# Halves of whole weight tiles made two products ahead in a hybrid decoder layer

## Chip, cores and metric

One core of a Trainium2 chip. The metric is the device time of one execution, in microseconds. A line of code is named L153 and so on, as the profile counts them in the kernel before; TensorE is PE, VectorE is DVE, ScalarE is ACT, GpSimd is POOL and SyncE is SP in the rows.

## What is computed

One decoder layer over 1024 tokens with 1024 channels in float32, with d = 512 for the two branches and 2816 for the up projection:

```python
h = rmsnorm(x, g_mix); z = h @ w_in
a = a_val * sigmoid(a_gt)
a = causal_dwconv(a, conv_a_w) + conv_a_b                 # 31 taps
y_a = silu(layernorm(a, ln_a_g, ln_a_b)) @ w_a_out
y_b = (sc_b * causal_dwconv(sc_c * sc_v, conv_b_w)) @ w_b_out   # 3 taps
x = x + (g_a * y_a + g_b * y_b) @ w_o                     # g_a, g_b: sigmoids from z
u = rmsnorm(x, g_ffn) @ w_up
f = gelu(causal_dwconv(u[:, :2816], conv_f_w) + conv_f_b) * u[:, 2816:]
x = x + f @ w_down
x = x + sigmoid(rmsnorm(x, g_ple) @ w_ple_gate) * (p @ w_ple)
return rmsnorm(x, g_final)
```

## The kernel before

Activations lie channels by tokens, in tiles of 128 channels by 1024 tokens. Every float32 operand of a product is written as a high half `hi` (a cast on ACT, L130) and a low half `lo = x - hi` (a subtraction on VectorE, L131), both by `halve`; a product is then three matmuls (hi·hi, hi·lo, lo·hi; `mm`, L143 to L153). SBUF is one pool of 54 tiles of 4 KB per partition (`NBIG`), from which activations, raw weights and their halves are taken.

The stages follow each other on TensorE: the start with the p @ w_ple products; the input projection as pairs of weight tiles (`Pair`, matmuls L601, copies L610, L617 and L623), each made with sums of halves of the weights; the w_b products of the second branch, one whole weight tile of 8 blocks (128x128) for two output tiles (`half_products`), evicted by a multiplication with a gate (L870); between the first and the third of them the LayerNorm of the first branch, with column sums by matmuls with a matrix of ones (`cs_mm`, L380 and L381), subtraction of the mean (L878), squares (L391) and their sum (L399), square root (L360), reciprocal (L363), scaling (L888), SiLU (L889); the four w_a products with evictions L902 and L903 and halves `m` of the result; the eight o products (`o_mm`, L928 to L930), evicted by an addition to x (`o_add`, L938), scaled (L939), squared (L945, L948) and summed by columns (`o_rstd`, L968); the up projection in pairs again; the down projection in three chunks of 8, 8 and 6 blocks (additions L1086); and the gate stage, w_pg products in three segments of 448, 320 and 256 columns (`Item`, gate L1125 and L1128). A whole product of 8 blocks and 1024 columns is 48 matmuls of 512 columns.

Weights go through the `Loader` (L155 to L276). `use` lists every use of a weight in the order of the program and adds up its cost in passes: 48 for a whole tile of 8 blocks, 12 for a use of a pair. At each use `get` first requests loads on SP's queue, in the order of cost less AHEAD, as long as they lie at most AHEAD passes ahead (`whole` tiles L207; of pairs L213, L217, and L222 to L224 with accumulating loads by POOL, L226). Then it writes the halves (`split`) of those weights that lie at most SPLIT passes ahead. Loads named in `held` wait: "up" is held from the o stage's start, and let go (`ld.held.clear()`, L1005) behind the product and evictions of o's last pair for the first 512 tokens.

An engine runs its instructions in order. The orders of TensorE and SP are written out in the program; on ACT, VectorE and POOL a scheduler orders them at build time, except in the start and the gate stage, where ACT and VectorE are written out too. So where a weight's halves stand on ACT and VectorE follows from where `get` writes them and from what the scheduler makes of it.

Of the kernel before, what the change touches and what calls it, by code (L numbers as in the profile page):

```python
# [13 lines left out]
PE = mybir.EngineType.PE  # L14
ACT = mybir.EngineType.Activation
DVE = mybir.EngineType.DVE
SP = mybir.EngineType.SP
# [5 lines left out]
DC = 512  # L23
# [41 lines left out]
NBIG = 54  # L65


AHEAD = {"whole": 120, "r": 110, "q": 100, "s": 150, "late": 200}
SPLIT = 40


@with_exitstack
def trunk_kernel(ctx, tc, xT, pT, par, w_in, w_a, w_b, w_o, w_up, w_dn, w_ple, w_pg, outT):
# [48 lines left out]
    def slot(name, dt=F32):  # L122
        return big.tile([P, T], dt, tag="u", name=name)
# [31 lines left out]
    class Loader:  # L155
# [39 lines left out]
        def sort(self):  # L195
            self.loads.sort(key=lambda x: self.cost[x[0]] - AHEAD[x[1]])
            self.pending = list(self.splits)
# [32 lines left out]
        def split(self, key, arg):  # L230
# [13 lines left out]
                hi, lo = split(t, "w_" + key[-1])  # L244
            self.done[key] = (hi, lo)

        def fetch(self, n):

            while self.loaded < n:
                self.load(*self.loads[self.loaded][1:])  # L250
                self.loaded += 1
# [6 lines left out]
        def get(self, load=True):  # L258
            i = self.at
            self.at += 1  # L260
            now = self.cost[i]
            while load and self.loaded < len(self.loads):
                n, kind, key, _ = self.loads[self.loaded]
                if n > i and (key[0] in self.held or self.cost[n] - now > AHEAD[kind]):
                    break
                self.fetch(self.loaded + 1)
            while self.pending and (
                self.pending[0][0] <= i or load and self.cost[self.pending[0][0]] - now <= SPLIT
            ):
                self.split(*self.pending.pop(0)[1:])  # L270
            key, side = self.uses[i]
            w = self.done[key]
            if side is not None and key[-1] != "q":
                c = slice(side * DC, (side + 1) * DC)
                w = tuple(x[:, c] for x in w)
            return w  # L276

    def block_order(n, head=1):

# [31 lines left out]
    ld = Loader()  # L311
# [20 lines left out]
        ld.add(w_pg[j], 8, kind="late")  # L332
    ld.sort()

    with tc.manual_schedule(engines={PE, SP}):
        ps_stack = ExitStack()
        psp = ps_stack.enter_context(tc.tile_pool(name="psp", bufs=8, space=PSUM))

# [216 lines left out]
        def right_sums(a0, a1, b0, b1):  # L555

            t13, t24 = slot("t13"), slot("t24")
            nc.vector.tensor_sub(t13[:, H0], a0, a1)
            nc.vector.tensor_sub(t13[:, H1], b1, a1)
            nc.vector.scalar_tensor_tensor(t24[:, H0], t13[:, H0], -1.0, b1, ALU.mult, ALU.subtract)  # L560
            nc.vector.scalar_tensor_tensor(t24[:, H1], t24[:, H0], -1.0, b0, ALU.mult, ALU.subtract)
            return t13, t24

        def sum_halves(t13, t24, name):

            out = {}
            hi, lo = split(t13, name + "s")
            out[5], out[7] = (hi[:, H0], lo[:, H0]), (hi[:, H1], lo[:, H1])
            hi, lo = split(t24, name + "t")
            out[6], out[4] = (hi[:, H0], lo[:, H0]), (hi[:, H1], lo[:, H1])  # L570
            return out
# [241 lines left out]
        for i in range(4):  # L813
            xa, xb = xr[i], xr[4 + i]
            r = sum_halves(*right_sums(xa[:, H0], xa[:, H1], xb[:, H0], xb[:, H1]), "hs")
# [14 lines left out]
        for n, (p, m) in enumerate(in_order):  # L830
            if m == 1:
                kind, i = IN_PAIRS[p]
# [109 lines left out]
        def o_square(i, c):  # L942
            r = xs[i, c.start]
            sq = slot("sq")
            nc.scalar.activation(sq, r, AF.Square)  # L945
            if c.start in osum:
                acc = osum[c.start]
                nc.vector.tensor_add(acc, acc, sq)  # L948
            else:
                osum[c.start] = sq  # L950

        def o_plain(i):

            hi, lo = split(xg[i, 0], "xgp")
            rows[i][1], rows[i][2] = (hi[:, H0], lo[:, H0]), (hi[:, H1], lo[:, H1])
# [8 lines left out]
        def o_rstd(c, cs):  # L964
            ps = bank()
            for i, q in enumerate(HALVES):
                for x, y in ((0, i == 0), (1, False)):
                    nc.tensor.matmul(ps, ones_d, cs[x][:, q], start=y, stop=x == 1 and i == 1)  # L968
            sqrt(rstd[:, c], ps)
            inverse(rstd[:, c])  # L970
# [24 lines left out]
        for i in (2, 3):  # L995
            for c in HALVES:
                for q in range(2):
                    if (i, c, q) == (3, H1, 1):
                        o_rstd(H0, cs_0)
                    o_mm(i + 4 * q, c, range(KD), True, True)  # L1000
                    o_add(i, q, c)
                if c is H0:
                    o_plain(i)
                if i == 3 and c is H0:
                    ld.held.clear()  # L1005
                    o_square(i, c)
                    cs_0 = cs_split(osum[0])
                    o_sums(2)
                elif i == 3:
                    o_sums(i)  # L1010
                    o_square(i, c)
                else:
                    o_square(i, c)
# [147 lines left out]
        with tc.manual_schedule(engines={ACT, DVE}):  # L1161
# [80 lines left out]
            fs, r = stats[-1]  # L1242
# [83 lines left out]
```

## Time and profile before

| | before |
|---|---|
| median of 3 runs | 1506.3 us (1506.01 to 1506.63) |
| profiled execution, its own time | 1504.43 us |
| its span | 1502.7 us |
| mean granted TensorE clock | 0.952 |
| TensorE busy | 1356.9 us, 90% of the span |
| VectorE busy | 913.4 us, 61% |
| ACT busy | 526.3 us, 35% |
| DMA | 216.64 MB, mean 144 GB/s |

The profile is of one execution; its own time is 1.9 us under the median of the runs, and 1.7 us lie around its span. A granted clock of 1.00 is 2.4 GHz, one of 0.50 is 1.2 GHz. "Idle before" is the time in which an engine did nothing ahead of an instruction, with the work whose end let it go. Some matmul records are missing in a trace, so counts of them are a little low.

### The profile page before, as it was taken

What the parts mean: (1) busy time and instruction counts of PE and PEld (TensorE: products, weight loads), DVE (VectorE), ACT (ScalarE), POOL (GpSimd) and SP (SyncE); (2) the same over time, 40 slices, a digit from 0 to 9 for tenths busy, and PEclk for the clock granted to TensorE, in tenths of its full rate; (3) what the DMA queues carried; (4) which work ended last, traced back from release to release, by engine and by line L of the source; (5) the groups of instructions that cost most, each with busy time, mean ns of one, the idle gap of its engine ahead of it and who ended that gap; (6) DMA issues with size and microseconds to landing.
All of it is one profiled execution on the core that took longest, in us unless ns stands there. A gap on an engine that the chain in (4) does not pass through costs nothing.

```text
span 1502.7 us, 15409 instructions
## 1 busy us (share of the span) xinstructions
PE 1356.9 (90%) x5930; PEld 1116.9 (74%) x5930; DVE 913.4 (61%) x1036; ACT 526.3 (35%) x691; POOL 181.7 (12%) x247
## 2 busy tenths in 40 slices
PE   9989999999839787768999999999979999997697
PEld 7778887888737566556888888888858888886586
DVE  7979999994463535355666666666674341254376
ACT  7442432344331124233433333333352120133244
POOL 1111321221000001013222222222000000000011
PEclk9999999999968989888999999999989999999798
DMA  9564876786732204048777777777392230112022
GB/s 340 146 137 123 247 180 147 189 215 185 275 144 79 89 0 140 28 134 188 182 182 182 182 178 180 182 182 182 106 381 81 90 107 11 61 53 84 18 77 78
DMA packets 84905, 216.64 MB, mean 144 GB/s; under 512 B 9696, under 2 KB 14048, under 8 KB 84832
## 3 DMA queue, kind: packets, MB, share of 16 engines
q1 hardware_dynamic: 52992, 140.15, 28.8%
q0 software_dynamic: 31840, 75.51, 21.8%
q8 instruction: 46, 0.75, 0.2%
q14 instruction: 27, 0.22, 0.1%
HBM read 159.00 MB, written 36.70 MB: 130 GB/s over the span
## 4 chain that ended last, share of the span: by engine, by line
PE 80%; DVE 11%; ACT 4%; issue 2%; DMA 2%; SPq 0%; DVEq 0%; ACTq 0%
PE ps L601 43%; PE ps L153 31%; PE ps L930 2%; PE ps L928 2%; DVE acc L676 2%; PE ps L929 2%; DVE wlo L131 1%; ACT whi L130 1%; DVE w_s_lo L131 1%; DVE ssq L399 1%; DMA x<-x_d 1%; DVE sc_cv L676 1%; DVE rstd L363 0%; DVE lrstd L363 0%; DVE w_r_lo L131 0%
## 5 line engine op out<-in xcount | busy, mean ns | idle before, releaser
L676 DVE SCALAR_TENSOR_TENSOR acc<-a,prm,acc 128x1023 f32<-128x1023 f32 (+14 forms) x120 | 151.7, 1264 | 1.7
L153 PE MATMUL ps<-f_hi,whi 128*128 128x512 f32 x352 | 109.2, 392 | 9.4 <-ACT whi L130 9.4
L153 PE MATMUL ps<-f_hi,wlo 128*128 128x512 f32 x352 | 108.9, 391 | 0.1
L153 PE MATMUL ps<-f_lo,whi 128*128 128x512 f32 x352 | 108.9, 390 | 0.0
L131 DVE TENSOR_TENSOR w_s_lo<-s,w_s_hi 128x1024 fp32r<-128x1024 f32 x76 | 92.5, 1219 | 16.1 <-DMA gate_d<-gate 8.4
L1086 DVE TENSOR_TENSOR x<-ps,x 128x512 f32<-128x512 f32 x46 | 29.6, 685 | 104.9 <-PE ps L153 104.9
L226 POOL DMA_DIRECT2D s<-s x76 | 66.6, 876 | 184.5 <-DMA s<-s 66.9
L153 PE MATMUL ps<-xp_hi,whi 128*128 128x448 f32 (+2 forms) x192 | 66.5, 347 | 24.1 <-ACT whi L130 22.9
L623 ACT COPY u<-ps 128x512 f32<-128x512 f32 x38 | 22.4, 589 | 182.5 <-PE ps L601 182.5
L131 DVE TENSOR_TENSOR wlo<-raw,whi 128x1024 fp32r<-128x1024 f32 (+2 forms) x55 | 63.0, 1160 | 34.9 <-ACT whi L130 17.8
L153 PEld LDWEIGHTS ps<-f_hi,whi 128*128 128x128 f32 x352 | 66.5, 189 | 23.6 <-ACT whi L130 9.9
L130 ACT CAST w_s_hi<-s 128x1024 fp32r<-128x1024 f32 x76 | 79.7, 1050 | 2.9 <-DMA s<-s 2.0
L601 PE MATMUL ps<-xgp_hi,w_r_hi 128*128 128x512 f32 x176 | 69.5, 395 | 12.0 <-ACT w_r_hi L130 12.0
L153 PEld LDWEIGHTS ps<-f_hi,wlo 128*128 128x128 f32 x352 | 66.2, 188 | 14.5 <-DVE wlo L131 0.9
L153 PEld LDWEIGHTS ps<-f_lo,whi 128*128 128x128 f32 x352 | 66.4, 189 | 14.0
L928 PE MATMUL ps<-m,whi 128*128 128x512 f32 x128 | 54.6, 426 | 22.8 <-ACT whi L130 22.8
L676 DVE SCALAR_TENSOR_TENSOR fg<-u_t,neg_f,fg 128x1023 f32<-128x1023 f32 (+1 forms) x44 | 56.4, 1283 | 28.3 <-ACT fg L670 27.6
L601 PE MATMUL ps<-xgp_hi,w_r_lo 128*128 128x512 f32 x176 | 69.4, 394 | 0.2 <-DVE w_r_lo L131 0.2
L601 PE MATMUL ps<-xgp_lo,w_r_hi 128*128 128x512 f32 x176 | 69.2, 393 | 0.0
L153 PE MATMUL ps<-xp_hi,wlo 128*128 128x448 f32 (+2 forms) x192 | 66.1, 344 | 3.1 <-DVE wlo L131 2.8
L601 PE MATMUL ps<-xgs_hi,w_s_hi 128*128 128x512 f32 x176 | 68.5, 389 | 0.0
L601 PE MATMUL ps<-xgs_lo,w_s_hi 128*128 128x512 f32 x176 | 68.5, 389 | 0.0
(263 smaller groups left out, 3366.5 us busy)
## 6 DMA issues: line engine op xcount, KB each, us to landing
s<-s POOLq DMA_DIRECT2D x76, 256.0 KB, 4.4
raw_r<-w_up SPq DMA_DIRECT2D x22, 512.0 KB, 5.2
s<-w_up SPq DMA_DIRECT2D x44, 256.0 KB, 3.0
s<-w_up SPq DMA_DIRECT2D x22, 512.0 KB, 6.0
s<-w_up POOLq DMA_DIRECT2D x44, 256.0 KB, 6.5
f_d<-v_t POOLq DMA_DIRECT2D x22, 512.0 KB, 5.9
f<-f_d SPq DMA_DIRECT2D x22, 512.0 KB, 5.2
s<-w_in SPq DMA_DIRECT2D x32, 256.0 KB, 3.0
```

The lines of the kernel that those rows point to most:

```text
L130: nc.scalar.copy(hi, src)
L131: nc.vector.tensor_sub(lo, src, f32(hi))
L153: nc.tensor.matmul(ps[:, :step], wt[:, b], xt[:, t : t + step], start=f, stop=l)
L226: nc.gpsimd.dma_start(dst, src, accum_op=ALU.add)
L399: nc.vector.tensor_add(self.acc[:, c], self.acc[:, c], sq[:, c])
L601: nc.tensor.matmul(ps, wt[:, b], xt, start=f, stop=l, skip_group_check=True)
L623: nc.scalar.copy(self.e[:, H1], self.b)
L676: nc.vector.scalar_tensor_tensor(dst[:, s:], src[:, : T - s], w(k), dst[:, s:], ALU.mult, ALU.add)
L928: nc.tensor.matmul(ps, whi[:, b], hi, start=first and k == ks[0], stop=False)
L929: nc.tensor.matmul(ps, whi[:, b], lo, start=False, stop=False)
L930: nc.tensor.matmul(ps, wlo[:, b], hi, start=False, stop=last and k == ks[-1])
L1086: nc.vector.tensor_add(x1[j][:, c], ps, x1[j][:, c])
```

## The change

Four things. SPLIT is now 100 passes for whole tiles (it was 40) and stays at 40 for pairs, with the condition that the raw tile has already been requested (`ready`). AHEAD for whole tiles goes from 120 to 150. The part of `get` that requests and splits is a method `advance` of its own, and it is called once more where the hold on up's loads ends. SP's order is no longer written out in the program but left to the scheduler.

```diff
--- before.py
+++ after.py
@@ -65,8 +65,8 @@
 NBIG = 54
 
 
-AHEAD = {"whole": 120, "r": 110, "q": 100, "s": 150, "late": 200}
-SPLIT = 40
+AHEAD = {"whole": 150, "r": 110, "q": 100, "s": 150, "late": 200}
+SPLIT = {True: 100, False: 40}
 
 
 @with_exitstack
@@ -244,6 +244,9 @@
                 hi, lo = split(t, "w_" + key[-1])
             self.done[key] = (hi, lo)
 
+        def ready(self, key):
+            return key in self.raw
+
         def fetch(self, n):
 
             while self.loaded < n:
@@ -258,22 +261,26 @@
         def get(self, load=True):
             i = self.at
             self.at += 1
+            self.advance(i, load)
+            key, side = self.uses[i]
+            w = self.done[key]
+            if side is not None and key[-1] != "q":
+                c = slice(side * DC, (side + 1) * DC)
+                w = tuple(x[:, c] for x in w)
+            return w
+
+        def advance(self, i, load=True):
             now = self.cost[i]
             while load and self.loaded < len(self.loads):
                 n, kind, key, _ = self.loads[self.loaded]
                 if n > i and (key[0] in self.held or self.cost[n] - now > AHEAD[kind]):
                     break
                 self.fetch(self.loaded + 1)
-            while self.pending and (
-                self.pending[0][0] <= i or load and self.cost[self.pending[0][0]] - now <= SPLIT
-            ):
+            while self.pending:
+                n, key, arg = self.pending[0]
+                if n > i and not (load and self.cost[n] - now <= SPLIT[key[0] == "whole"] and self.ready(key)):
+                    break
                 self.split(*self.pending.pop(0)[1:])
-            key, side = self.uses[i]
-            w = self.done[key]
-            if side is not None and key[-1] != "q":
-                c = slice(side * DC, (side + 1) * DC)
-                w = tuple(x[:, c] for x in w)
-            return w
 
     def block_order(n, head=1):
 
@@ -332,7 +339,7 @@
         ld.add(w_pg[j], 8, kind="late")
     ld.sort()
 
-    with tc.manual_schedule(engines={PE, SP}):
+    with tc.manual_schedule(engines={PE}):
         ps_stack = ExitStack()
         psp = ps_stack.enter_context(tc.tile_pool(name="psp", bufs=8, space=PSUM))
 
@@ -1003,6 +1010,7 @@
                     o_plain(i)
                 if i == 3 and c is H0:
                     ld.held.clear()
+                    ld.advance(ld.at - 1)
                     o_square(i, c)
                     cs_0 = cs_split(osum[0])
                     o_sums(2)
```

TensorE's order is the same. At three places the others stand as follows; `whi` and `wlo` are the halves of a whole weight tile, `raw` the loaded tile, `cs_hi` and `cs_lo` the halves of what is summed over columns.

First, ACT at the end of the input projection and at the LayerNorm's sums. Before:

```order
L623 COPY u_2858<-ps 128x512
L783 ACTIVATE gate<-gate,prm 128x512
L783 ACTIVATE gate<-ps,prm 128x512
L130 CAST s_hi<-s 128x1024
L783 ACTIVATE gate<-gate,prm 128x512
L130 CAST s_hi<-s 128x1024
L130 CAST cs_hi<-acc 128x1024
L391 ACTIVATE ssq<-acc 128x1024
L391 ACTIVATE sq<-acc 128x1024 x3
L130 CAST cs_hi<-ssq 128x1024
L130 CAST whi<-raw 128x1024
L360 ACT_TABLE_LOAD
```

and now:

```order
L130 CAST whi<-raw 128x1024
L630 COPY u_2860<-ps 128x512
L790 ACTIVATE gate<-gate,prm 128x512
L790 ACTIVATE gate<-ps,prm 128x512
L130 CAST s_hi<-s 128x1024
L790 ACTIVATE gate<-gate,prm 128x512
L130 CAST s_hi<-s 128x1024
L130 CAST cs_hi<-acc 128x1024
L130 CAST whi<-raw 128x1024
L398 ACTIVATE ssq<-acc 128x1024
L398 ACTIVATE sq<-acc 128x1024 x3
L130 CAST cs_hi<-ssq 128x1024
```

The second w_b's cast stood behind the second column sum's (`cs_hi<-ssq`); it is now ahead of the last copy of the pairs, and the third's stands ahead of the squares. In VectorE's order at the same place, before:

```order
L870 TENSOR_TENSOR gate<-ps,gate 128x512 x4
L878 TENSOR_TENSOR acc<-acc,ps 128x512 x8
L399 TENSOR_TENSOR ssq<-ssq,sq 128x1024 x3
L131 TENSOR_TENSOR cs_lo<-ssq,cs_hi 128x1024
L131 TENSOR_TENSOR wlo<-raw,whi 128x1024
L870 TENSOR_TENSOR gate<-ps,gate 128x512 x4
L363 RECIPROCAL lrstd<-lrstd 128x512 x2
L888 TENSOR_TENSOR acc<-acc,lrstd 128x1024 x4
```

and now:

```order
L877 TENSOR_TENSOR gate<-ps,gate 128x512 x4
L885 TENSOR_TENSOR acc<-acc,ps 128x512 x8
L877 TENSOR_TENSOR gate<-ps,gate 128x512 x2
L131 TENSOR_TENSOR wlo<-raw,whi 128x1024
L406 TENSOR_TENSOR ssq<-ssq,sq 128x1024 x2
L877 TENSOR_TENSOR gate<-ps,gate 128x512
L406 TENSOR_TENSOR ssq<-ssq,sq 128x1024
L877 TENSOR_TENSOR gate<-ps,gate 128x512
L131 TENSOR_TENSOR cs_lo<-ssq,cs_hi 128x1024
L131 TENSOR_TENSOR wlo<-raw,whi 128x1024
L370 RECIPROCAL lrstd<-lrstd 128x512 x2
L877 TENSOR_TENSOR gate<-ps,gate 128x512
```

The evictions `gate<-ps` of the second product (two, then one and one) now stand among the additions of squares, ahead of the column sum's low half.

Second, VectorE at the first square sum of o (`x<-ps` is an eviction of a product, `sq<-sq` the addition of squares, `t` the first of the sums for up). Before:

```order
L938 TENSOR_TENSOR x_3949<-ps,x_3949 128x512
L131 TENSOR_TENSOR xgp_lo<-xg,xgp_hi 128x1024
L948 TENSOR_TENSOR sq<-sq 128x1024
L938 TENSOR_TENSOR x_3952<-ps,x_3952 128x512
L131 TENSOR_TENSOR cs_lo<-sq,cs_hi 128x1024
L558 TENSOR_TENSOR t_4167<-xg 128x512
```

and now:

```order
L945 TENSOR_TENSOR x_3959<-ps,x_3959 128x512 x2
L131 TENSOR_TENSOR xgp_lo<-xg,xgp_hi 128x1024
L945 TENSOR_TENSOR x_3962<-ps,x_3962 128x512
L955 TENSOR_TENSOR sq<-sq 128x1024
L131 TENSOR_TENSOR cs_lo<-sq,cs_hi 128x1024
L565 TENSOR_TENSOR t_4189<-xg 128x512
```

The addition of squares stood ahead of the eviction to `x_3952`, the first of the last residual tile, and now stands behind that eviction (to `x_3962`, the same tile).

Third, ACT in the gate stage (L1128 is the sigmoid, L1139 and L1141 squares, L1147 the scaled output; the line numbers of the changed kernel are 7 or 8 higher there). Before:

```order
L130 CAST whi<-raw 128x1024
L360 ACTIVATE rstd_8729<-ps_8796,eps_t 128x448
L360 ACTIVATE rstd_8729<-ps_8828,eps_t 128x320
L360 ACTIVATE rstd_8729<-ps_8832,eps_t 128x256
L130 CAST whi<-raw 128x1024
L1128 ACT_TABLE_LOAD
L1128 ACTIVATE last<-last 128x448 x2
L1139 ACTIVATE fs<-x_7285 128x448
L1128 ACTIVATE last<-last 128x448
L1147 ACTIVATE x_7285<-x_7285,prm 128x448
L1141 ACTIVATE last<-x_7287 128x448
L130 CAST whi<-raw 128x1024
```

and now:

```order
L130 CAST whi<-raw 128x1024 x2
L367 ACTIVATE rstd_8733<-ps_8804,eps_t 128x448
L367 ACTIVATE rstd_8733<-ps_8836,eps_t 128x320
L367 ACTIVATE rstd_8733<-ps_8840,eps_t 128x256
L130 CAST whi<-raw 128x1024
L1136 ACT_TABLE_LOAD
L1136 ACTIVATE last<-last 128x448 x2
L1147 ACTIVATE fs<-x_7289 128x448
L1136 ACTIVATE last<-last 128x448
L1155 ACTIVATE x_7289<-x_7289,prm 128x448
L1149 ACTIVATE last<-x_7291 128x448
L130 CAST whi<-raw 128x1024
```

Two casts of weights now stand ahead of the square roots, where one stood; each later one comes one item earlier.

## Rows read from the trace of the kernel before

**Rows 1.** Waits of TensorE: waiter, releaser, us in total, times, longest.

```profile
PE ps L153 <- ACT whi L130: 75.7, 13, 18.9
PE ps L928 <- ACT whi L130: 22.8, 5, 9.9
PE ps L601 <- ACT w_r_hi L130: 12.0, 1, 12.0
```

**Rows 2.** Busy windows by stage: stretch, length, busy of each engine, PEclk, DMA.

```profile
397.18:545.39 148.21, 100.31 (x393) 80.10 (x391) 77.91 (x90) 36.87 (x45) 0.53 (x1) 0.85 0.33 118
545.39:680.00 134.61, 101.35 (x389) 78.73 (x389) 59.24 (x65) 44.91 (x53) 12.21 (x20) 0.85 0.28 94
1099.00:1121.00 22.00, 11.49 (x42) 8.34 (x43) 18.01 (x18) 13.50 (x14) 0.53 (x1) 0.79 1.02 408
1121.00:1360.00 239.00, 237.75 (x1049) 196.63 (x1048) 87.36 (x100) 50.59 (x53) 0.00 (x0) 1.00 0.25 82
1358.23:1438.44 80.21, 54.21 (x198) 44.46 (x199) 32.38 (x40) 22.67 (x35) 0.00 (x0) 0.83 0.11 33
```

**Rows 3.** Timeline of TensorE, behind gaps: start, duration, instruction, [idle before].

```profile
419.97 0.79 PE L153 MATMUL ps<-s_hi,whi 128*128 128x512 f32 x1 [10.83 <-ACT whi L130]
453.56 0.80 PE L153 MATMUL ps<-s_hi,whi 128*128 128x512 f32 x1 [18.90 <-ACT whi L130]
493.81 1.22 PE L153 MATMUL ps<-an_hi,whi 128*128 128x512 f32 x2 [4.53 <-ACT whi L130]
680.00 0.80 PE L601 MATMUL ps<-xgp_hi,w_r_hi 128*128 128x512 f32 x1 [12.01 <-ACT w_r_hi L130]
1118.02 1.22 PE L153 MATMUL ps<-f_hi,whi 128*128 128x512 f32 x2 [9.44 <-ACT whi L130]
1405.81 0.74 PE L153 MATMUL ps<-xp_hi,whi 128*128 128x448 f32 x1 [3.99 <-ACT whi L130]
```

**Rows 4.** Busy windows right behind two gaps (columns as in the windows above).

```profile
419.97:425.30 5.33, 5.33 (x13) 4.16 (x14) 1.40 (x2) 1.25 (x1) 0.00 (x0) 0.50 0.98 389
511.07:513.50 2.43, 2.43 (x6) 1.95 (x7) 1.20 (x1) 0.00 (x0) 0.00 (x0) 0.50 0.58 179
```

**Rows 5.** Timelines of SP and ACT: last w_a load, and its cast.

```profile
433.31 0.33 SPq L207 DMA_DIRECT2D raw<-w_a  x1
527.22 1.04 ACT L130 CAST whi<-raw 128x1024 fp32r<-128x1024 f32 x1
```

**Rows 6.** Timelines of VectorE and ACT around the LayerNorm's second column sum.

```profile
414.02 3.88 DVE L399 TENSOR_TENSOR ssq<-ssq,sq 128x1024 f32<-128x1024 f32 x3
417.93 1.04 ACT L130 CAST cs_hi<-ssq 128x1024 fp32r<-128x1024 f32 x1 [2.74 <-DVE ssq L399]
419.01 1.23 DVE L131 TENSOR_TENSOR cs_lo<-ssq,cs_hi 128x1024 fp32r<-128x1024 f32 x1 [1.11 <-ACT cs_hi L130]
434.23 1.27 ACT L360 ACTIVATE lrstd<-ps,eps_t 128x512 f32<-128x512 f32 x2 [13.01 <-PE ps L381]
```

**Rows 7.** Timelines of VectorE, SP and ACT at the end of o.

```profile
659.61 0.69 DVE L938 TENSOR_TENSOR x<-ps,x 128x512 f32<-128x512 f32 x1 [0.51 <-PE ps L930]
662.31 0.33 SPq L213 DMA_DIRECT2D raw_r<-w_up  x1
678.90 1.99 ACT L130 CAST w_r_hi<-raw_r 128x1024 fp32r<-128x1024 f32 x2
```

**Rows 8.** Timeline of ACT at the end of up.

```profile
1113.15 3.87 ACT L130 CAST f_hi<-f 128x1024 fp32r<-128x1024 f32 x4
1116.93 2.94 ACT L130 CAST whi<-raw 128x1024 fp32r<-128x1024 f32 x3
```

**Rows 9.** Timeline of TensorE, last product of the gate stage's first segment.

```profile
1436.99 0.37 PE L153 MATMUL ps<-xp_hi,wlo 128*128 128x448 f32 x1
1438.44 0.31 PE L153 MATMUL ps<-xp_hi,whi 128*128 128x320 f32 x1
```

**Rows 10.** DMA issues: line, KB each, median us from issue to landing.

```profile
raw<-w_dn SPq DMA_DIRECT2D x16, 512.0 KB, 5.4
```

## The prediction

> **What bounds the kernel now.** I read the waits of TensorE first [rows 1]: each row is a line of matmuls, what ended its idle time, the sum, how often, and the longest. By far the largest sum, 75.7 us in 13 waits, is products of whole weight tiles (line 153) waiting for ACT's cast that makes a weight tile's high half (line 130); the o products (line 928) wait 22.8 us for the same cast, and one wait of 12.0 us stands before the up projection. Then the windows by stage [rows 2]: the stages of pairs and the down projection lose nothing (237.75 us busy of 239 at a granted clock of 1.00, and 1049 matmuls there give 0.2266 us each, 10.88 us for a whole weight's 48), but the branch stage (w_b, w_a) has 100.31 us of work in 148.21, the o stage with the way to up 101.35 in 134.61, the gate stage 54.21 in 80.21. The timeline of TensorE [rows 3] shows where: before nearly every whole product stands a gap, each released by that cast. The gap costs twice: behind it the granted clock is 0.50, which is 1.2 GHz, for 5.33 us in one case and 2.43 us in another [rows 4], before it is back near 1.00. Work at half speed for so long loses half of it, so a removed gap gives back its length and 1.2 to 2.7 us more.
>
> Why the cast is late: not for want of data. The last w_a tile was requested at 433.31 and its cast began at 527.22 [rows 5]. ACT works in order, the cast is written behind the casts of `m`, and those wait for the end of the product before. That order is what the change moves.
>
> **The change, part by part.**
>
> *Halves two products ahead.* SPLIT goes from 40 passes to 100 for whole tiles, and a whole product counts 48: before, the cast of the next weight was written during the product just ahead of it; now it is written up to two products ahead, where TensorE's last product does not release it. No arithmetic is added or taken away.
>
> Term 1, branch stage, from 397.18 to 545.39, 148.2 us. Eight products at 10.88 are 87.0, the eight column-sum matmuls 1.8 (0.2266 each): 88.8 us if nothing waits. One wait is new. The second w_b's halves are now ready when the first product ends, at 409.1 (419.97 less its gap of 10.83 [rows 3]), so it ends at about 420.0. The column sums of the LayerNorm stand behind it on TensorE, and before they were ready in the gap (low half from 419.01 on [rows 6]). Now VectorE has two evictions of the second product between the additions of squares: the last of the first kind ends at about 420.4, the third addition takes 1.3 (3.88 for three [rows 6]), then cast 1.04 and low half 1.23, so 424.2: a wait of 4.2 us, and with 2 us of clock behind it the third w_b ends at about 438, the fourth at 449.2. Behind the sums stands the chain to the normalized activations: before it took 19.3 us from the square root at 434.23 [rows 6] to the matmul at 453.56 [rows 3]; from about 426 on, with three evictions more in it, its low halves and the first w_a's are there at about 447, two microseconds before they are wanted. The four w_a products follow without a gap, and w_o begins at 492.7 instead of 545.39. **Gain 52.7.** Bounds: if the new wait hides, 59; if chain or evictions cost 4.5 us (the gap of today [rows 3]) on each of the four w_a products, 35.
>
> Term 2, o stage, from 545.39 to the end of its last product at 668.0 (680.00 less 12.01), 122.6 us. Eight products are 87.0, the first square-sum's four matmuls 0.9. New is again a wait at the sum: VectorE's order puts the addition of squares behind an eviction that waits for the product just ahead of the sum on TensorE, so the sum waits 0.69 (eviction [rows 7]) + 1.3 + 1.04 + 1.23 = 4.3, and 1.5 of clock: 93.5 in all. **Gain 29.1**; without that wait 34, with the waits of the last four weights kept (22.8 less the first one's 4.5 [rows 1]) 11.
>
> *Up's first weights requested when their hold ends.* Today they are requested from 662.31 on and cast at 678.90 [rows 7]. Between lie ACT's casts of the last o outputs and the second square sum; the w_r cast is behind them in the order of after too. So the earlier request is hidden by ACT's queue, and the gap of 12.0 stays. **Gain 0**; bounds 0 to +10, if the casts should slip ahead.
>
> Term 3, end of up. TensorE runs the first two blocks of the first w_down weight and waits 9.44 us to 1118.02 [rows 3]. Now the second weight's halves are also made before the last copy of up: its two blocks, 12 matmuls, fill 2.7 us of the gap, and ACT has three casts instead of four before the next weight's [rows 8], so TensorE resumes 1 us sooner. **Gain 3.7.** The window 1099 to 1121 has DMA at a share of 1.02 and 408 GB/s [rows 2]: if the w_down tile lands late, 0; if all four weights' first blocks could run, 9. The Trainium skill (DMA: Bandwidth & Descriptors, Issuing engines are not separate DMA queues) states that whatever engine starts a transfer, it runs on the same 16 DMA engines; by it moving requests earlier there gives nothing, and the sum would be 121.1 instead of 124.8. The row agrees that they are full in these 22 us, but the second w_down tile is requested long before.
>
> Term 4, gate stage, first column segment, from 1358.23 to 1438.44, 80.2 us. 448-column matmuls at full clock follow each other every 0.207 us (seven in 1.45 [rows 9]); 192 of them are 39.7, the norm's few about 1: 40.6. Each w_pg half is written two items ahead of the item that needs it, so the gaps of 4.0 us [rows 3] close. **Gain 39.6.** Cover: VectorE has 32.38 us of work in the stage [rows 2], which must fit in 40.6; in its new order each low half stands two or three microseconds before its matmul. If that cover goes, each of seven items waits about 1.2 us and keeps some clock loss: 30.
>
> *SP's order left to the scheduler.* The order of loads on SP changes little: parameters are the first load, one w_o earlier, four w_down behind the x1 loads. The first x loads move back by one small transfer; its issue is 0.33 us (as one issue in [rows 5]). **Cost 0.3**; bounds 0 to 1. The pair halves keep 40, and their stages have no gap to lose.
>
> Sum: 52.7 + 29.1 + 0 + 3.7 + 39.6 − 0.3 = 124.8 off the profiled execution's 1504.43, which gives 1379.6. The profiled execution is 1.9 under the median of the runs, 1506.3; on the median's footing the forecast is **1381.5 us**.
>
> **The rivals.**
>
> *Another wait takes the place (chance 0.08).* VectorE's low halves could queue behind evictions that wait for the product just ahead. Then 16 of the 24 products (w_a, the last four of o, the gate stage) would still wait for eviction, addition and low half, about 0.69 + 0.69 + 1.23 = 2.6 us, with 1.3 of clock: 62 us come back, 1444 us. For it: VectorE is the second engine of these stages and works in order; the two new waits above are of this kind. Against it: in the new order the low halves stand ahead of the evictions of the product under way.
>
> *Up's gap closes too (0.03):* the profile's 12.0 less some 2 that stay, 1371.5.
>
> *The change doesn't do what it says (0.02):* halves are made ahead only where the raw tile has been requested; if this held them back, or ACT's order kept them behind, about 1506. Against: the w_a request 94 us before its cast [rows 5].
>
> *Slower, by tiles (0.02).* Halves made two products earlier hold four more of the 54 tiles. In the down stage a weight's load could then wait for a free tile, and the whole way would lie in front of each product: landing 5.4 [rows 10], cast 1.04, low half 1.23, some 7.7 us × 24 products = 185 us, less 124.8 gained: 1566 us. It decides when a w_down tile is requested later than 3.2 us (10.88 − 7.7) after the start of the product before its own. For it: the same gap, 4.5 us, stands before three of the four w_a products. The Trainium skill (Perfetto Trace Analysis, Optimization Strategy) says that such consistent bubbles can mean there isn't enough SBUF or PSUM for the next tile, which would make this change wrong here. The trace speaks against it: the tile was there 94 us early, and the releaser is ACT's cast.
>
> **How the numbers follow.** Forecast 0.85, and the four rivals as above. The range goes from 1368 (up's gap closed and half of term 1's new wait hidden: 10 and 3 less) to 1410 (the lower bounds of terms 2 and 4 together, 18 and 10 more; those of terms 1 and 3 give 1403), and leaves out the rivals with 1444, 1506 and 1566. A difference under 0.2% can't be told from none. Faster: 0.85 + 0.08 + 0.03 = 0.96; same 0.02; slower 0.02.
>
> **What would show it.** Right: no wait for a weight cast before a w_b, w_a or o product; a new wait of about 4 us before the LayerNorm's second column sum and before the first square sum of o; the 12 us before up unchanged; about 5.5 us at the first w_down products; the gate stage's first segment near 41 us at a clock near 1.00. Wrong: repeating waits on VectorE's low halves, loads of w_down late in the down stage, or new gaps among the pairs.

## Result, and the profile after

The changed kernel takes 1381.04 us (median of 4 runs, 1380.39 to 1382.68) against 1506.47 us for the kernel before in the same series: a ratio of 0.9167, with a 95% interval of 0.9151 to 0.9183. The forecast was 1381.5 us. The profiled execution took 1381.46 us, with a span of 1379.5 us and a mean granted clock of 0.983 (0.952 before).

The first part of the page, busy time of each engine, and the clock's row of its second part, in 40 slices:

```profile
PE 1327.5 (96%) x5930; PEld 1102.4 (80%) x5930; DVE 911.6 (66%) x1036; ACT 526.3 (38%) x691; POOL 181.6 (13%) x247
...
PEclk9999999999999999989999999999999999999999
```

TensorE has the same 5930 matmuls, but 1327.5 us of them in place of 1356.9, since fewer run at half the clock. The other engines do what they did.

The waits of TensorE that the change bears on, the answer to [rows 1]: waiter, releaser, us in total, times, longest. (Two rows of the pairs between them, 4.0 and 3.5 us, are as before.)

```profile
PE ps L608 <- ACT w_r_hi L130: 11.7, 1, 11.7
PE ps L153 <- ACT whi L130: 5.8, 1, 5.8
PE ps L975 <- ACT cs_hi L130: 3.0, 1, 3.0
PE ps L387 <- ACT cs_hi L130: 2.8, 1, 2.8
```

Whole products waited 75.7 us in 13 waits for the cast of their weight; now there is one such wait, of 5.8 us, at the first w_down products. The o products don't wait for it at all. Two waits are new or longer: 3.0 us at o's first square sum (L975; 0.7 us before) and 2.8 us at the LayerNorm's second column sum (L387; none before). The wait before up, 12.0 us, is 11.7.

The windows of the stages, the answer to [rows 2]: stretch, length, busy time of each engine, granted clock, share of DMA, GB/s.

```profile
398.87:494.09 95.22, 91.99 (x394) 75.24 (x392) 74.16 (x86) 35.90 (x42) 0.53 (x1) 0.96 0.52 192
494.09:599.85 105.76, 90.28 (x389) 73.72 (x388) 60.43 (x68) 45.04 (x54) 16.45 (x26) 0.94 0.43 128
1274.69:1315.25 40.56, 40.56 (x198) 37.03 (x199) 30.88 (x39) 21.75 (x34) 0.00 (x0) 1.00 0.24 72
```

From the first w_b to the first o matmul it was 148.21 us and is 95.22; from there to up 134.61 and now 105.76; the gate stage's first segment 80.21 and now 40.56, with TensorE busy all the time at a clock of 1.00.

The timeline of TensorE at the gaps that are left: start, duration, instruction, idle time before it and its releaser.

```profile
424.50 0.79 PE L387 MATMUL ps<-cs_hi,ones_c 128*128 128x512 f32 x1 [2.77 <-ACT cs_hi L130]
425.76 0.80 PE L388 MATMUL ps<-cs_lo,ones_c 128*128 128x512 f32 x1 [0.47 <-DVE cs_lo L131]
578.84 0.51 PE L975 MATMUL ps<-cs_hi,ones_d 128*128 128x512 f32 x1 [2.99 <-ACT cs_hi L130]
580.10 0.50 PE L975 MATMUL ps<-cs_lo,ones_d 128*128 128x512 f32 x1 [0.76 <-DVE cs_lo L131]
599.85 0.79 PE L608 MATMUL ps<-xgp_hi,w_r_hi 128*128 128x512 f32 x1 [11.74 <-ACT w_r_hi L130]
1036.91 0.79 PE L153 MATMUL ps<-f_hi,whi 128*128 128x512 f32 x1 [5.78 <-ACT whi L130]
```

By term, in the two profiled executions:

| term | forecast | measured | how |
|---|---|---|---|
| start and pairs | −0.3 | −1.7 | first w_b at 397.18, then 398.88 |
| 1, branch | 52.7 | 53.0 | 148.21 − 95.22 |
| 2, o | 29.1 | 28.6 | 122.60 − (599.85 − 11.74 − 494.09 = 94.02) |
| before up | 0 | 0.3 | 12.01 − 11.74 |
| 3, up and down | 3.7 | 3.4 | (1358.23 − 680.00) − (1274.69 − 599.85) |
| 4, gate stage | 39.6 | 39.65 | 80.21 − 40.56 |
| sum | 124.8 | 123.2 | 1502.7 − 1379.5 |

### The profile page after: what moved, and what is told of

The parts are those of the page before. It is cut to its first block, busy times and chain, and to the rows that moved or that the text cites. A ratio compares the mean times of both kernels' runs of the same rounds, so it can differ in the third digit from the quotient of the medians.

```text
span 1379.5 us, 15421 instructions
## 1 busy us (share of the span) xinstructions
PE 1327.5 (96%) x5930; PEld 1102.4 (80%) x5930; DVE 911.6 (66%) x1036; ACT 526.3 (38%) x691; POOL 181.6 (13%) x247
## 4 chain that ended last, share of the span: by engine, by line
PE 86%; DVE 7%; ACT 2%; DMA 2%; issue 2%; SPq 0%; DVEq 0%; ACTq 0%
PE ps L608 47%; PE ps L153 33%; DVE acc L683 2%; PE ps L937 2%; PE ps L936 2%; PE ps L935 2%; DVE w_s_lo L131 1%; DMA x<-x_d 1%; DMA f<-f_d 1%; DVE sc_cv L683 1%; DVE ssq L406 0%; DVE w_r_lo L131 0%; DMA p_raw<-pT 0%; ACT ple_o L452 0%; DMA x_raw<-xT 0%
## 5 line engine op out<-in xcount | busy, mean ns | idle before, releaser
L608 PE MATMUL ps<-xgp_hi,w_r_hi 128*128 128x512 f32 x176 | 69.4, 394 | 11.7 <-ACT w_r_hi L130 11.7
L608 PE MATMUL ps<-xgs_hi,w_s_lo 128*128 128x512 f32 x176 | 68.5, 389 | 0.0
L130 ACT CAST whi<-raw 128x1024 fp32r<-128x1024 f32 (+2 forms) x55 | 53.9, 999 | 37.5 <-PE ps L153 28.3
L153 PE MATMUL ps<-xp_hi,whi 128*128 128x448 f32 (+2 forms) x192 | 61.5, 320 | 1.2 <-ACT sq L398 1.2
```

The costliest lines, as they stand in the source:

```text
L130: nc.scalar.copy(hi, src)
L153: nc.tensor.matmul(ps[:, :step], wt[:, b], xt[:, t : t + step], start=f, stop=l)
L608: nc.tensor.matmul(ps, wt[:, b], xt, start=f, stop=l, skip_group_check=True)
```

## Experiments

Each kernel was timed beside the kernel before, whose medians in these series lie between 1505.75 and 1506.17 us.

**The new SPLIT alone.** The other three parts are taken back.

```diff
-AHEAD = {"whole": 150, "r": 110, "q": 100, "s": 150, "late": 200}
+AHEAD = {"whole": 120, "r": 110, "q": 100, "s": 150, "late": 200}
-    with tc.manual_schedule(engines={PE}):
+    with tc.manual_schedule(engines={PE, SP}):
-                    ld.advance(ld.at - 1)
```

> Only the new SPLIT with its condition; AHEAD stays 120, nothing is requested at the end of the hold, and SP keeps the program's order. Theory (halves): the whole gain comes from the casts and subtractions of whole tiles standing further ahead on ACT and VectorE, so nearly all of it is here: 1380 us, 1377 to 1386, with no wait for a whole weight's cast in the stages of w_b, w_a, o and the gate. The start loses its 1.7 us of delay, since the parameters are no longer the first load. Rival (loads): earlier requests are what closes the gaps; then half of the gain or less is here, 1440 us or more.

Measured: 1385.03 us (1383.20 to 1386.18), a ratio of 0.9193 (0.9178 to 0.9209). So 121 us of the 125 come from SPLIT alone, and the rival that credits earlier loads falls. It was not quite without waits, though. The timeline of TensorE at the first w_a product, in this kernel:

```profile
451.97 0.73 PE L153 MATMUL ps<-an_hi,whi 128*128 128x512 f32 x2 [3.52 <-ACT whi L130]
456.00 1.22 PE L153 MATMUL ps<-an_hi,wlo 128*128 128x512 f32 x2 [2.44 <-DVE wlo L131]
```

Six microseconds of wait for the first w_a weight's halves stand here that the changed kernel doesn't have. In exchange the wait at o's first square sum is as small as before (0.66 and 0.76 us). The start was not faster than in the changed kernel: its first pairs begin at 86.45 us as they did before, but 1.5 us are lost again by 146 us.

**SPLIT taken back, the rest kept.**

```diff
-SPLIT = {True: 100, False: 40}
+SPLIT = {True: 40, False: 40}
```

> The changed kernel with SPLIT back at 40 for whole tiles; AHEAD 150, the request at the end of the hold and the scheduler's order of loads stay. Theory (halves): no gain is left, and the start's delay of 1.7 us shows alone: 1506 to 1510 us, with the same sums of waits for casts as before (about 76 us on whole products, 23 on o). Rival (loads): 1450 us or less.

Measured: 1512.58 us (1510.93 to 1512.78), a ratio of 1.0040 (1.0026 to 1.0055): slower than the kernel before, and 2.6 us above the end of what was expected. The waits of TensorE in this kernel:

```profile
PE ps L153 <- ACT whi L130: 73.8, 13, 17.6
PE ps L935 <- ACT whi L130: 22.9, 5, 10.0
PE ps L975 <- ACT cs_hi L130: 3.0, 1, 3.0
```

The waits for weights are back nearly whole, 73.8 and 22.9 us, and the new wait at o's square sum is here without any halves made ahead. It belongs to the other parts of the change. So they cost by themselves: with SPLIT at 40 some 6 to 7 us (6.0 by the ratio, 6.8 between the medians), of which the stretch from the first o matmul to up (134.61 before, 138.30 here) holds 3.7. Three runs narrow down which part that is: the same stretch is 105.76 us in the changed kernel, 105.77 with SP's order written out and 105.77 with AHEAD back at 120 (both below), and 102.08 in the run with SPLIT alone. So the part that is left is the extra request where the hold ends, though no run takes that back alone.

**SP's order written out again.**

```diff
-    with tc.manual_schedule(engines={PE}):
+    with tc.manual_schedule(engines={PE, SP}):
```

> The changed kernel, but SP's order is the program's again. ACT, VectorE and POOL keep the order of the changed kernel; on SP only the load of the parameters moves back from the first place to behind the first x tiles. Theory: 0.5 us of the start's 1.7 come from that load's issue in front of all others, and the other 1.2 from where the granted clock falls: 1379.3 to 1380.8 us, the first products of the pairs about 0.5 to 1.7 us earlier. Rival (the scheduler's order of loads is worth something): 1383 us or more. Rival (the load's place plays no part): 1381 us, the start as late as in the changed kernel.

Measured: 1382.10 us (1381.16 to 1383.77), 0.9178 (0.9164 to 0.9191): the same as the changed kernel within the intervals. The first rows of SP's timeline in this kernel show the parameters back behind the x tiles:

```profile
0.74 0.38 SPq L431 DMA_DIRECT2D p_raw<-pT  x1
3.54 6.46 SPq L435 DMA_DIRECT2D x_raw<-xT  x8
10.35 0.33 SPq L480 DMA_DIRECT2D prm<-par  x1
```

Still the first column sum comes at 41.66 and the first pairs' wait at 88.80 (41.23 and 88.11 in the changed kernel). My theory for the start falls: the place of that load is not what costs 1.7 us, and the part of the change that frees SP is worth nothing that can be measured. Nor is 1.7 us a fixed cost: in three kernels whose ACT and SP follow the same order there, the first pairs begin at 86.71 (one product ahead), 88.11 (the changed kernel) and 89.18 us (the LayerNorm's sum later), against 86.31 before.

**One product ahead in place of two.**

```diff
-SPLIT = {True: 100, False: 40}
+SPLIT = {True: 60, False: 40}
```

> The changed kernel with SPLIT at 60 for whole tiles, so that halves are made one product ahead and not two. Theory: what counts is that the cast is no longer behind the evictions of the product just ahead of it; one product ahead is enough for that, and only around the LayerNorm's chain may the fourth w_b's halves come late, by up to 10 us: 1381 to 1395 us. Rival (two products are needed): gaps of 2 us and more come back before most whole products, 1420 us or more.

Measured: 1401.76 us (1400.65 to 1404.38), 0.9310 (0.9296 to 0.9324). Neither: one product ahead gives five sixths of the gain (104 of 125 us). Its timeline of TensorE has three places where the cast is late again:

```profile
444.17 1.22 PE L153 MATMUL ps<-s_hi,whi 128*128 128x512 f32 x2 [5.65 <-ACT whi L130]
554.97 0.50 PE L935 MATMUL ps<-m,whi 128*128 128x512 f32 x1 [4.58 <-ACT whi L130]
1296.74 0.47 PE L153 MATMUL ps<-xp_hi,whi 128*128 128x448 f32 x1 [1.91 <-ACT whi L130]
```

Those are products whose cast falls behind a chain: the LayerNorm's (the fourth w_b, as expected), that of o's first outputs and that of the gate stage's first square sums. Before most products one ahead is enough.

**Three products ahead.**

```diff
-SPLIT = {True: 100, False: 40}
+SPLIT = {True: 150, False: 40}
```

> The changed kernel with SPLIT at 150 for whole tiles, halves up to three products ahead. Theory: only the gap of 5.8 us before the first w_down products still waits for a whole weight's cast, so at most that closes: 1375 to 1382 us. Rival (casts of weights made too early stand in front of what the chains need, on ACT and VectorE): longer waits at the sums of LayerNorm or o, 1384 us or more.

Measured: 1386.85 us (1386.58 to 1388.29), 0.9211 (0.9198 to 0.9225): slower than with two, as the rival has it. The timeline of TensorE:

```profile
428.04 0.79 PE L387 MATMUL ps<-cs_hi,ones_c 128*128 128x512 f32 x1 [6.02 <-ACT cs_hi L130]
501.95 0.50 PE L936 MATMUL ps<-m,whi 128*128 128x512 f32 x1 [2.57 <-DVE m L131]
1046.25 1.22 PE L153 MATMUL ps<-f_hi,whi 128*128 128x512 f32 x2 [4.88 <-ACT whi L130]
```

The wait at the LayerNorm's second sum is 6.0 us in place of 2.8, one of 2.6 us stands at the start of o, and the gap before w_down is only 0.9 us smaller. But what holds up the sum is not a cast standing in front of it, which was the rival's reason. VectorE's timeline in this kernel, at the sum and at the start of o:

```profile
421.83 1.29 DVE L877 TENSOR_TENSOR gate<-ps,gate 128x512 f32<-128x512 f32 x2 [3.02 <-PE ps L153]
423.04 3.88 DVE L406 TENSOR_TENSOR ssq<-ssq,sq 128x1024 f32<-128x1024 f32 x3
500.08 1.22 DVE L131 TENSOR_TENSOR wlo<-raw,whi 128x1024 fp32r<-128x1024 f32 x1
```

All three additions of squares stand behind the last two evictions of the second w_b product, for which VectorE waits idle; in the changed kernel two of the three stand ahead of them. At the start of o a weight's low half, 1.22 us, does stand in front of the low halves of `m`, behind the evictions of the last w_a product. So what costs here is mainly the order that the scheduler makes on VectorE with the halves written earlier, and only in a small part the early halves' own time.

**AHEAD alone taken back.**

```diff
-AHEAD = {"whole": 150, "r": 110, "q": 100, "s": 150, "late": 200}
+AHEAD = {"whole": 120, "r": 110, "q": 100, "s": 150, "late": 200}
```

> The changed kernel with AHEAD for whole tiles back at 120. With SPLIT alone a new wait of 3.5 and 2.4 us stood before the first w_a product, which the changed kernel doesn't have. Theory (AHEAD at 150 matters only by the order that the scheduler then makes on VectorE, where loads come earlier in its reckoning): that wait is here again, 1385 us, 1382 to 1388. Rival (the scheduler's order of loads or the request at the end of the hold removes it): 1379 to 1382 us.

Measured: 1388.18 us (1387.13 to 1389.99), 0.9221 (0.9206 to 0.9237), a little above the expected range. The waits of 3.52 and 2.31 us before the first w_a product are there again. VectorE's timeline behind the LayerNorm's second sum, first in this kernel and then in the changed one:

```profile
430.20 0.69 DVE L877 TENSOR_TENSOR gate<-ps,gate 128x512 f32<-128x512 f32 x1 [6.31 <-PE ps L153]
432.54 6.55 DVE L370 RECIPROCAL lrstd<-lrstd 128x512 f32<-128x512 f32 x2
452.98 1.21 DVE L131 TENSOR_TENSOR wlo<-raw,whi 128x1024 fp32r<-128x1024 f32 x1
```

```profile
427.43 6.56 DVE L370 RECIPROCAL lrstd<-lrstd 128x512 f32<-128x512 f32 x2 [0.59 <-ACT lrstd L367]
447.08 1.21 DVE L131 TENSOR_TENSOR wlo<-raw,whi 128x1024 fp32r<-128x1024 f32 x1
```

The reciprocals stand behind an eviction that waits for the third w_b product, and begin at 432.54, 5.1 us later than in the changed kernel; the chain behind them, and the first w_a weight's low half at its end, are later by 5 to 6 us. So AHEAD at 150 is worth some 7 us here by the order that the scheduler then makes. Loads that land earlier are not what does it: in this kernel ACT runs without idle time from 440.80 to the casts of the w_a weights at 449.13, and from the reciprocals to that low half VectorE waits only for ACT's halves (0.33 and 0.85 us), so nothing there waits for a load.

**Six tiles fewer.**

```diff
-NBIG = 54
+NBIG = 48
```

> The changed kernel with 48 tiles in the pool in place of 54. The halves made ahead hold four tiles more than before, so if tiles had become scarce, six fewer would show. Theory (tiles don't bound): 1379 to 1388 us, no wait of loads that reaches TensorE in the down stage; the orders of VectorE differ in some places, which may cost a few us. Rival (tiles are at their limit): loads of whole tiles come late, gaps of several us before down products, 1400 us or more.

Measured: 1381.66 us (1380.82 to 1385.20), 0.9182 (0.9162 to 0.9202): no change. TensorE's waits are those of the changed kernel (11.7, 5.8, 3.0 and 2.8 us). Tiles do not bound this kernel, and the repeating gaps were not a shortage of buffers: with more tiles held and fewer to hold them they are gone. The rule of the Trainium skill (Perfetto Trace Analysis, Optimization Strategy) that the prediction weighed says only that they can mean that; here the order of one feeding engine made them.

**The LayerNorm's second sum later.** Its matmuls stand between the two halves of the third w_b product.

```diff
-            for j, g, pss in zip((jj, 4 + jj), gs[jj], half_products(s_t)):
+            for j, g, pss in zip((jj, 4 + jj), gs[jj], half_products(s_t, normalize if jj == 2 else None)):
...
             for i in range(2):
+                if i and between:
+                    between()
```

> The changed kernel with the LayerNorm's second column sum placed on TensorE between the two halves of the third w_b product, 24 matmuls later. Theory (the new wait of 3.2 us there is the sum standing too early, and nothing behind it needs it so soon): the wait and about 1.3 us of clock behind it go, 1376.5 us, 1374 to 1379. Rival (the chain to the w_a products bounds this stretch): the first w_a product waits as much as was saved, 1380 to 1383 us.

Measured: 1383.79 us (1382.91 to 1384.34), 0.9188 (0.9175 to 0.9202). The wait at the sum is gone, and two others stand at the first w_a product, as the rival has it. TensorE's timeline, then rows of ACT and VectorE:

```profile
448.79 0.78 PE L153 MATMUL ps<-an_hi,whi 128*128 128x512 f32 x2 [2.90 <-ACT an_hi L130]
451.77 0.80 PE L153 MATMUL ps<-an_lo,whi 128*128 128x512 f32 x1 [2.21 <-DVE an_lo L131]
429.13 1.27 ACT L367 ACTIVATE lrstd<-ps,eps_t 128x512 f32<-128x512 f32 x2
434.82 1.29 DVE L892 TENSOR_TENSOR gate<-ps,gate 128x512 f32<-128x512 f32 x2 [3.95 <-PE ps L153]
437.15 6.56 DVE L370 RECIPROCAL lrstd<-lrstd 128x512 f32<-128x512 f32 x2
```

The products now wait 5.1 us for the normalized activations: from the first w_b to the first w_a it is 48.45 us in place of 51.69, and from there to o 48.21 in place of 43.52. But the chain does not come late because of the sum's new place. The square roots end at 430.4, and the reciprocals begin only at 437.15, since the scheduler put them behind evictions of the third w_b product, for which VectorE waits, and a low half. In the changed kernel they begin 0.7 us behind the start of the square roots. VectorE is free at 430.9, so begun then they would be 6.3 us earlier (an estimate from these rows), which is more than the 5.1 us. So this run shows that the later place gains nothing with the order that the scheduler makes of it; what the wait at the sum costs by itself stays open.

**The square sum of o first, as before the change.** The orders of ACT and VectorE in the last third of o are written out.

```diff
+        with tc.manual_schedule(engines={ACT, DVE}):
+            o_plain(3)
+            o_square(3, H0)
+            cs_0 = cs_split(osum[0])
+            o_sums(2)
...
```

> The changed kernel, with the orders of ACT and VectorE in the last third of o written out: the addition of squares stands ahead of the eviction of the next product again, as before the change. Theory (the new wait for o's first square sum is that one place in VectorE's order): the wait of 3.7 us and about 1.5 us of clock go, the 11.7 us before up stay within 1 us: 1376 us, 1373 to 1379. Rival (what is saved there is lost in the gap before up, which ends with ACT's and VectorE's chain of the last o product): 1380 to 1383 us.

Measured: 1380.86 us (1379.72 to 1382.84), 0.9168 (0.9152 to 0.9185), no change, as the rival has it. TensorE at the sum and before up, and VectorE's reciprocal:

```profile
575.72 0.50 PE L975 MATMUL ps<-cs_hi,ones_d 128*128 128x512 f32 x1 [0.66 <-ACT cs_hi L130]
598.77 0.80 PE L608 MATMUL ps<-xgp_hi,w_r_hi 128*128 128x512 f32 x1 [15.34 <-ACT w_r_hi L130]
585.86 3.35 DVE L370 RECIPROCAL rstd<-rstd 128x512 f32<-128x512 f32 x1 [2.79 <-ACT rstd L367]
589.13 0.63 DVE L945 TENSOR_TENSOR x<-ps,x 128x512 f32<-128x512 f32 x1
```

The wait at the sum falls to 0.66 and 0.76 us, and the gap before up grows from 11.74 to 15.34. TensorE ends the last o product 4.7 us earlier than in the changed kernel (583.43 for 588.11), but VectorE's last eviction, behind the reciprocal, ends at 589.8, only 1.0 us earlier than there (590.8). From there the chain of sums and casts leads to up's first weight. The order that was written out has a part in this: it also puts the next eviction behind the sums for up (582.38 us, for 575.88 in the changed kernel), and the square root, on whose end the reciprocal waits, behind that (585.14, though the sum's matmuls ended at 577.95). So the run shows that the saved time is lost in this order, not that it would be in every one.

**Up's first halves where the hold ends.**

```diff
                     ld.advance(ld.at - 1)
+                    ld.split_to(ld.at + 2)
```

> The changed kernel, with the halves of up's first two pair weights also written where the hold ends, not in front of up's first product. On ACT their casts now stand ahead of the squares of o's last pair. Theory (ACT's order ends the gap before up, not the loads): the gap of 11.7 us goes; the two low halves stand ahead of the addition of squares on VectorE, so the wait for the first square sum grows by 2.4 us: 1371 us, 1367 to 1376. Rival (the load or the free tile ends the gap): 1379 to 1383 us.

Measured: 1370.31 us (1369.48 to 1371.05), 0.9099 (0.9086 to 0.9113): faster than the changed kernel by 10.7 us. The waits of TensorE have no row for `w_r_hi` any more. The one at the square sum:

```profile
PE ps L975 <- ACT cs_hi L130: 5.8, 2, 5.3
```

The wait at the sum is 5.3 us in place of 3.0, as expected. So the gap before up was ACT's order, and neither load nor tiles. In the changed kernel the first of these tiles is requested at 554.12 and cast at 598.76:

```profile
554.12 0.33 SPq L213 DMA_DIRECT2D raw_r<-w_up  x1
598.76 1.99 ACT L130 CAST w_r_hi<-raw_r 128x1024 fp32r<-128x1024 f32 x2
```

**The same one product earlier.** The hold ends and the halves are written ahead of the last product for o's first 512 tokens.

```diff
+                    if (i, c, q) == (3, H0, 1):
+                        ld.held.clear()
+                        ld.advance(ld.at - 1)
+                        ld.split_to(ld.at + 3)
...
-                    ld.held.clear()
-                    ld.advance(ld.at - 1)
```

> The changed kernel with up's first loads let go one product earlier and the halves of up's first two pair weights written there, ahead of the eviction on which the first square sum waits. Theory: the low halves no longer delay the square sum by 2.3 us, and the gap before up is gone: 1369 us, 1366 to 1371. Rival (the stretch is bound by VectorE's work, whichever way it is ordered): the same as with the halves one product later, 1370 to 1372 us.

Measured: 1369.49 us (1368.69 to 1371.93), 0.9097 (0.9083 to 0.9110). The wait at the sum is 4.18 us in place of 5.32, half of what was expected, since the low half `xgp_lo` now stands behind the eviction. The intervals of this and the last kernel overlap: it can't be told which is right.

**Both: the sum's order, and up's halves early.** ("The last" below is the kernel with the square sum of o first.)

```diff
+            ld.split_to(ld.at + 2)
+            o_part(3, H1)
+            o_sums(3)
...
+            if n == 2:
+                o_rstd(H0, cs_0)
```

> As the last, and besides the halves of up's first two pair weights written ahead of the last evictions of o, and the first square sum's matmuls moved behind up's first two products. Theory: the wait at the sum and the gap before up both go, 3.7 + 11.7 us and their clock, less a few us where up meets the second square sum: 1365 us, 1362 to 1369, faster than the changed kernel with the early halves alone (1370.3). Rival (up's next step then waits for the second square sum and the sums of halves, which the last o product's chain makes): 1369 to 1373 us.

Measured: 1371.37 us (1367.38 to 1372.65), 0.9099 (0.9080 to 0.9118). The rival's side: no better than the early halves alone. TensorE leaves o at 581.9 and starts up at 583.52, but then waits in up. Its timeline, and a row of VectorE's:

```profile
583.52 0.50 PE L608 MATMUL ps<-xgp_hi,w_r_hi 128*128 128x512 f32 x1 [1.62 <-ACT w_r_hi L130]
607.47 0.65 PE L608 MATMUL ps<-xgs_hi,w_s_lo 128*128 128x512 f32 x1 [3.09 <-DVE w_s_lo L131]
599.17 6.56 DVE L370 RECIPROCAL rstd<-rstd 128x512 f32<-128x512 f32 x2 [0.59 <-ACT rstd L367]
```

The 3.09 us are for a low half behind the two reciprocals, 6.56 us on VectorE. From 580 to 600 VectorE is busy for 17.2 us of 20. From the first o matmul to up it is 88.82 us, 7.7 less than with the early halves alone (96.51), but the up projection behind it, to the first w_down matmul, is 430.95 for 425.06, 5.9 more: most of what was saved comes back one stage later.

The best kernels of this study are those with up's first halves early, at 1369.5 and 1370.3 us.

## Why the prediction was right, and where not

*What bounds.* Right. The cast of a weight stood behind the casts of `m` in ACT's order, not behind a load: SPLIT alone gives 121 of the 125 us, and without it nothing is gained. One sentence of the prediction was loose: before, a weight's halves were written only when its own product came, since one product ahead is 48 passes and SPLIT was 40. The rows and the terms were read from the trace and don't hang on it.

*Term 1, branch:* 53.0 for 52.7. The new wait was forecast at 4.2 us until 424.2 and stood at 2.77 and 0.47 us, until 425.8; the first product of the stage began 1.7 us later. VectorE's rows show the forecast order at work: the eviction at 421.55, the third addition, the eviction, the low half.

```profile
421.55 0.69 DVE L877 TENSOR_TENSOR gate<-ps,gate 128x512 f32<-128x512 f32 x1 [0.56 <-PE ps L153]
422.15 1.22 DVE L406 TENSOR_TENSOR ssq<-ssq,sq 128x1024 f32<-128x1024 f32 x1
423.29 0.69 DVE L877 TENSOR_TENSOR gate<-ps,gate 128x512 f32<-128x512 f32 x1
424.48 1.22 DVE L131 TENSOR_TENSOR cs_lo<-ssq,cs_hi 128x1024 fp32r<-128x1024 f32 x1 [0.51 <-ACT cs_hi L130]
```

The bound of 59 for a hidden wait was not tested: the experiment with the later sum hides the wait, but loses the time again by VectorE's order.

*Term 2, o:* 28.6 for 29.1, with a wait of 2.99 and 0.76 us where 4.3 were forecast. Its bound of 34 without the wait holds inside the term: with the square sum first, the o products take 90.12 us (493.31 to 583.43), 32.5 less than before, with 1.4 us of wait left. But what is saved there came back before up, which the bound didn't count.

*Up's early request:* right for the gap, 12.01 and now 11.74, and the reason was tested. That the request costs nothing was not right, as far as the runs can tell: by elimination it is what puts the eviction ahead of the addition of squares, and the stretch from o to up is 3.7 us longer with it. The prediction had read that order and counted its wait in term 2, without asking which part made it. The rival that this gap closes too needed its halves to be written early, which the change doesn't do.

*Term 3:* 3.4 for 3.7. TensorE resumes with 5.78 us of gap where some 5.5 were forecast. *Term 4:* 39.65 for 39.6.

*The start* was mis-sized: 0.3 us forecast, bounds 0 to 1, and 1.7 measured in the profiled executions. The reason, the parameters' load ahead of all others, was wrong as well, as the run with SP's old order shows. With one profile of each kernel, and the first pairs between 86.71 and 89.18 us in kernels with the same orders there, the part of it that is the change's own can't be told. At the same first gap of the start the clock behaved differently; the windows right behind it, of the kernel before and of the changed one:

```profile
40.75:44.00 3.25, 3.02 (x12) 2.29 (x13) 3.17 (x5) 1.24 (x2) 0.00 (x0) 1.00 1.03 415
```

```profile
41.23:44.00 2.77, 2.71 (x6) 1.85 (x7) 2.69 (x5) 1.24 (x2) 0.00 (x0) 0.53 1.03 411
```

Behind 2.69 us of gap the clock stayed at 1.00 there, behind 2.25 us it is 0.53 here, which costs some 1.3 us. In the run with SPLIT alone the same gap leaves it at 1.00, and 1.5 us are lost later. What decides this was not found.

*The sum.* Two of the prediction's additions are off by 0.2 us: 420.4 + 1.3 + 1.04 + 1.23 is 424.0, not 424.2 (term 1), and 87.0 + 0.9 + 4.3 + 1.5 is 93.7, not 93.5 (term 2, 28.9). The 4.5 us of the first o product's wait, put down to [rows 1], stand in the trace at 545.39 and not in those rows. The sum came to 123.2 us in the profiled executions for 124.8. That the forecast median is within 0.5 us of the measured one is partly chance: the profiled execution before was 2.0 us under its median, the one after 0.4 over, which covers the start's error.

*The rivals.* Another wait in the place of the old ones: only two, of 3 us each. No effect, and too few tiles: out by the runs above.

## What to carry to other kernels

A gap that repeats before every product, released by a cheap instruction whose data came long before, is an order on the feeding engine: write that instruction ahead of what waits for the last product. How far ahead has an optimum (here two products: 1381 us; one 1402, three 1387), because each step also changes the order on the engines that feed the chains: look there at what a chain's next instruction stands behind. A short wait in such a chain is worth removing only after what comes next has been looked at: two waits of 3 us were each moved away here, and neither gave anything, both times because a reciprocal or an eviction on VectorE then stood in a worse place. Whether another order would keep the gain stays open.

## What had not been expected

The three small parts cost 6 to 7 us without SPLIT and AHEAD's is worth 7 us with it, with the same number of instructions on every engine: each part's worth depends on the order that the scheduler makes of all of them. At the same gap of the start the granted clock behind it was 1.00 in the three kernels where the gap was longest (2.68 to 2.71 us: before, SPLIT alone, one product ahead), and 0.50 to 0.70 in the eleven others, with gaps of 2.19 to 2.50 us. So a longer gap did not cost more here; the windows are the 2.8 us behind the gap.
